# A two-layer hybrid decoder trunk on one core: the up product in its own buffer, and the probabilities' transposes and pooling products one step later

## The chip, the core and the metric

The kernel runs on one core of a Trainium2 chip. PE multiplies matrices, DVE and ACT work elementwise, GpSimd (POOL) does a few masks, and DMA queues move data, nearly all of them issued by SyncE (SP). Each engine takes its instructions in a fixed order and waits on semaphores for what other engines produce. The metric is the device time of one execution in microseconds (us); the time before is the median of three runs.

## The reference

Two layers run over 256 tokens of width 1024, all in float32. Cut to what matters here:

```python
def swiglu(x, w_gate, w_up, w_down):
    return (jax.nn.silu(x @ w_gate) * (x @ w_up)) @ w_down
...
for i in range(DEPTH):                                   # 2
    h = h + 0.5 * swiglu(rmsnorm(h, ffn1_norm[i]), ...)  # 1024 -> 2816 -> 1024
    u = rmsnorm(h, mix_norm[i])
    (q, c_kv, q_idx, w_idx, k_idx, x_pool, z, xbc, dt_raw, gate_raw) = jnp.split(u @ w_in[i], offs, axis=-1)
    y_attn = dsa_attention(...)   # indexer picks 64 of the causal keys; 8 heads: scores, softmax, values
    y_pool = pool_mixer(x_pool, pool_w[i], pool_scale[i])   # 4 groups: trailing mean minus x, times a 128x128 matrix
    y_ssd = ssd_mixer(...)        # convolution, chunked scan, gate
    merged = (g_attn * (y_attn @ w_br_attn[i]) + g_pool * (y_pool @ w_br_pool[i]) + g_ssd * (y_ssd @ w_br_ssd[i]))
    h = h + merged @ w_out[i]
    h = h + 0.5 * swiglu(rmsnorm(h, ffn2_norm[i]), ...)
    h = h + jax.nn.sigmoid(rmsnorm(h, ple_norm[i]) @ ple_w_gate[i]) * (p[i] @ ple_w_proj[i])
return rmsnorm(h, final_norm)
```

## The kernel before

Channels lie on partitions and tokens along the free dimension, so a product with 128 output channels is a matmul of a 128x128 weight tile against 128x256 activations. To keep float32 accuracy every operand is split into a high part and a low part of a shorter type (whi and wlo, uh and ul, gh and gl), and a product is the sum of three: high by high (L211), low of the activations by high of the weights (L212), high by low of the weights (L213).

Weights come in units of 128x1024. `load` (L141) issues the unit's transfer on SP into raw (L144), lets ACT cast the high part (L145) and DVE subtract it for the low part (L146). Raw has four buffers, whi and wlo five each. `unit` asks for a number of units ahead of the one in use (AHEAD, usually four). The low parts carry a mark ("turn"), and marked DVE instructions keep the order in which the program writes them. Everything else is put in order when the program is built, by a list scheduler that goes by its own estimates and by priorities; PE instructions issued through `self.mm` and `self.transpose` keep the program's order among themselves, other matmuls are placed freely. What results is one fixed order for each engine.

**FFN.** `ffn` goes over 22 pairs f of a gate and an up product, each of 24 matmuls, into the two halves of one PSUM bank (four banks called mm serve them in turn). For each pair DVE multiplies the gate product by the norm's factor (L494, out of PSUM), ACT takes a tanh (L498), DVE multiplies the same buffer by the up product (L500, out of PSUM, in place, after the tanh has read it), adds and multiplies (L501), and `split` makes gh and gl (L250, L251). A bank is free for a later pair when L500 has read it. In the very first FFN the norm's factor comes late (`todo`), so the first pairs wait together in a list. A small table there says how many units are asked for ahead of each unit.

**Mix.** Four generators are woven into one program: the state-space branch, the attention, the pooling branch and the gates' products. `weave` gives each a start, a number of steps and an end, and takes the next step from the one that is least far; a bare `yield` in a generator is an empty step that lets the others go on. In the attention `softmax` takes maxima (L896, DVE), exponentials (L898, ACT) and scalings of the probabilities (L902, ACT), lets 4 - h steps pass (h is the half of the queries), transposes them on PE (L114) and copies them out (L914). Where attention and state-space branch meet, `self.hold` is set to 4: that many of the next weight products (in groups of four tiles) are kept in program order behind what stands before them; others may be moved ahead by the scheduler. In the pooling branch each group's sum is split (L250, L251) and, two steps later, multiplied by its 128x128 matrix (po).

Of the kernel before, what the change touches and what calls it, by code (L numbers as in the profile page):

```python
# [13 lines left out]
OP = mybir.AluOpType  # L14
# [54 lines left out]
class Builder:  # L69
# [374 lines left out]
    def ffn(self, layer, u0, nxt, aside=None):  # L444
# [6 lines left out]
        for f in range(KF):  # L451
# [7 lines left out]
            elif f == 0:  # L459
                ps = [self.bank(t)[:, :S] for t in ("mm", "aux")]  # L460
                for c in range(KD):
                    for i, j in ((0, 0), (0, 1), (1, 0)):
                        for k, p in enumerate(ps):
                            nc.tensor.matmul(p, self.w01[i][:, c, k * P:(k + 1) * P], u[j][:, c],
                                             start=c + i + j == 0, stop=c == KD - 1 and i == 1)
                self.later()
                self.later()
            else:
                ps = self.bank()
                ps = [ps[:, :S], ps[:, S:]]  # L470
                for j in range(2):
                    n = 2 * f + j
                    ahead = self.AHEAD
                    if u0 == U_FFN1:
                        ahead = {2: 2, 3: 2, 4: 1}.get(n, ahead) if first else \
                            {2: 2, 3: 2}.get(n, ahead)
                    w = self.unit(layer, u0 + n, 1024, ahead=ahead)
                    keep = j == 0 and f == (2 if first else 1)
                    mid = u0 == U_FFN1 and n == (4 if first else 2)
                    if first and f < 4:  # L480
                        self.mmk_late(ps[j], w, u, keep, mid)
                    else:
                        self.mmk([(ps[j], w)], u, keep=keep, mid=mid)
# [5 lines left out]
            waiting.append((f, ps))  # L489
            if self.todo is None:  # L490
                for f1, p1 in waiting:
                    t = self.t([P, S], tag="t1")
                    with self.tc.high_priority(offset=160):
                        ins = nc.vector.tensor_tensor(t, p1[0], r, op=OP.mult)  # L494
                    if f1 == 0:
                        self.turn(ins)
                    th = self.t([P, S], tag="t1")
                    nc.scalar.activation(th, t, AF.Tanh, scale=0.5)  # L498
                    g = self.t([P, S], tag="t1")
                    nc.vector.tensor_tensor(t, t, p1[1], op=OP.mult)  # L500
                    nc.vector.scalar_tensor_tensor(g, th, 1.0, t, op0=OP.add, op1=OP.mult)  # L501
                    self.split(gh[:, f1], gl[:, f1], g)
                waiting = []
        self.new_u()
# [56 lines left out]
    def mix(self, layer, nxt):  # L561
# [180 lines left out]
                    yield from self.pool_group(layer, i + j, px[:, j], wpl, yp)  # L742

        with self.tc.issue_after(self.last.ins):
            self.weave((states(), 55, 1), (attend(), 36, 1), (pools(), 22, 0.88), (gate, 48, 1.1),
                       apart=(0, 1))
        ysh, ysl, rs = res["ssd"]

# [134 lines left out]
    def softmax(self, h, two, mb, out):  # L883
# [6 lines left out]
        for ps, _ in two:  # L890
# [11 lines left out]
                nc.scalar.mul(pr[:, j], pr[:, j], sums[:, j:j + 1])  # L902
            prs.append(pr)
            yield
        for _ in range(4 - h):
            yield
        pts = [self.bank("aux") for _ in prs]
        for pt, pr in zip(pts, prs):
            for j in range(4):
                self.transpose(pt[:, j * P:(j + 1) * P],  # L910
                               pr[:, j // nb, (j % nb) * P:(j % nb + 1) * P], self.ident)
        for (_, heads), pt in zip(two, pts):
            th = self.t([P, 4, P])
            nc.scalar.copy(th, pt.rearrange("p (a b) -> p a b", a=4))  # L914
            out.append((heads, th))
            yield
# [214 lines left out]
    def pool_group(self, layer, g, x, wpl, yp):  # L1131
# [16 lines left out]
        yh = self.t([P, S], FR, tag="t1")  # L1148
        yl = self.t([P, S], FR, tag="t1")
        self.split(yh, yl, y)  # L1150
        yield
        yield
        po = self.bank()
# [284 lines left out]
```

## Time and profile before

| | before |
|---|---|
| median of three runs | 1308.79 us (1307.43 to 1309.79) |
| the profiled execution | 1307.58 us, span 1305.7 us |
| granted TensorE clock | 0.999 |
| PE busy | 1295.8 us, 99% |
| DVE busy | 1048.6 us, 80% |
| ACT busy | 739.6 us, 57% |
| moved by DMA | 248.41 MB, mean 190 GB/s |

The page gives averages over the span. PE runs nearly without a gap, so the page alone tells little of a change of a few microseconds; the timelines of single stretches tell more. In them a row is: start in us, length in us, engine, line, operation, what is written from what, shape, how many in a row, and in brackets the idle time before it with what ended it.

### The profile page before, as it was taken

The page shows a single profiled execution, that of the slowest core. Times are in us where ns is not written, and L with a number is a line of the kernel's source. Part 1 is how long each engine was busy: PE and PEld are TensorE (multiplying, and loading weights), DVE is VectorE, ACT ScalarE, POOL GpSimd, SP SyncE. Part 2 cuts the span into 40 slices and gives each one's busy share as a digit, 9 for nine tenths or more (in the row PEclk, how much of TensorE's full clock was granted, in tenths as well). Part 3 has the DMA queues.
Part 4 walks back from the last instruction along what each step waited for, and adds up shares of the span by engine and source line. Part 5 has one row for each costly group of instructions (what it writes and reads, how often), then busy time and mean ns, then how long its engine had stood idle before and what let it go on. Part 6 is the DMA issues. An engine that isn't in the chain of part 4 may idle for free.

```text
span 1305.7 us, 28173 instructions
## 1 busy us (share of the span) xinstructions
PE 1295.8 (99%) x11468; PEld 1288.0 (99%) x11468; DVE 1048.6 (80%) x1919; ACT 739.6 (57%) x1203; POOL 7.0 (1%) x17
## 2 busy tenths in 40 slices
PE   9999999999999999999999999999999999999998
PEld 9999999999999999999999999999999999999997
DVE  7877669987999887766887776799789989777667
ACT  6555446656864555544655554566577646555455
POOL 0000000000000000000000000000000000000000
PEclk9999999999999999999999999999999999999999
DMA  7666656566546576666656666555555566666661
GB/s 267 212 194 194 195 166 207 181 189 206 171 159 217 166 225 195 194 194 194 194 178 207 192 196 192 162 195 187 189 199 167 176 203 212 195 194 195 194 192 66
DMA packets 72242, 248.41 MB, mean 190 GB/s; under 512 B 7920, under 2 KB 10416, under 8 KB 72112
## 3 DMA queue, kind: packets, MB, share of 16 engines
q1 hardware_dynamic: 71680, 245.82, 59.4%
q8 instruction: 90, 1.47, 0.5%
q10 hardware_dynamic: 432, 0.79, 0.2%
q14 instruction: 40, 0.33, 0.1%
HBM read 245.50 MB, written 1.08 MB: 189 GB/s over the span
## 4 chain that ended last, share of the span: by engine, by line
PE 97%; DVE 1%; DMA 1%; ACT 1%; issue 0%; SPq 0%; DVEq 0%; ACTq 0%
PE mm L212 30%; PE mm L213 30%; PE mm L211 30%; PE aux L111 3%; DMA raw<-in_w_dram 1%; PE aux L213 1%; PE aux L212 1%; PE aux L114 1%; PE aux L211 1%; DVE wlo L146 0%; PE mm L111 0%; PE mm L547 0%; ACT whi L145 0%; PE mm L247 0%; ACT t L343 0%
## 5 line engine op out<-in xcount | busy, mean ns | idle before, releaser
L145 ACT CAST whi<-raw 128x1024 fp32r<-128x1024 f32 (+1 forms) x456 | 475.0, 1045 | 472.2 <-issue 207.8
L146 DVE TENSOR_TENSOR wlo<-raw,whi 128x1024 fp32r<-128x1024 f32 (+1 forms) x456 | 551.5, 1214 | 179.9 <-ACT whi L145 178.7
L212 PE MATMUL mm<-ul,whi 128*128 128x256 f32 x2454 | 676.9, 277 | 0.0
L213 PE MATMUL mm<-uh,wlo 128*128 128x256 f32 x2454 | 676.6, 277 | 0.0
L211 PE MATMUL mm<-uh,whi 128*128 128x256 f32 x2419 | 667.2, 277 | 2.2 <-DVE t L500 2.2
L212 PEld LDWEIGHTS mm<-ul,whi 128*128 128x128 f32 x2454 | 460.6, 188 | 0.0
L213 PEld LDWEIGHTS mm<-uh,wlo 128*128 128x128 f32 x2454 | 459.8, 188 | 0.1
L211 PEld LDWEIGHTS mm<-uh,whi 128*128 128x128 f32 x2419 | 453.1, 188 | 2.9 <-DVE t L500 2.4
L213 PE MATMUL mm<-gh,wlo 128*128 128x256 f32 x704 | 194.4, 276 | 0.0
L212 PE MATMUL mm<-gl,whi 128*128 128x256 f32 x704 | 194.4, 276 | 0.0
L211 PE MATMUL mm<-gh,whi 128*128 128x256 f32 x704 | 193.9, 276 | 0.0
L213 PEld LDWEIGHTS mm<-gh,wlo 128*128 128x128 f32 x704 | 132.2, 188 | 0.0
L212 PEld LDWEIGHTS mm<-gl,whi 128*128 128x128 f32 x704 | 132.2, 188 | 0.0
L211 PEld LDWEIGHTS mm<-gh,whi 128*128 128x128 f32 x704 | 131.9, 188 | 0.0
L212 PE MATMUL mm<-a,whi 128*128 128x256 f32 x256 | 70.8, 276 | 0.0
L213 PE MATMUL mm<-a,wlo 128*128 128x256 f32 x256 | 70.8, 276 | 0.0
L211 PE MATMUL mm<-a,whi 128*128 128x256 f32 x256 | 70.7, 276 | 0.0
L211 PEld LDWEIGHTS mm<-a,whi 128*128 128x128 f32 x256 | 48.1, 188 | 0.0
L212 PEld LDWEIGHTS mm<-a,whi 128*128 128x128 f32 x256 | 48.1, 188 | 0.0
L213 PEld LDWEIGHTS mm<-a,wlo 128*128 128x128 f32 x256 | 48.1, 188 | 0.0
L494 DVE TENSOR_TENSOR t<-mm,rs_r 128x256 f32<-128x256 f32 x88 | 37.3, 423 | 9.8 <-PE mm L213 0.6
L501 DVE SCALAR_TENSOR_TENSOR t<-t,t 128x256 f32<-128x256 f32 x88 | 37.4, 425 | 2.9
(292 smaller groups left out, 1245.6 us busy)
## 6 DMA issues: line engine op xcount, KB each, us to landing
raw<-in_w_dram SPq DMA_DIRECT2D x446, 512.0 KB, 4.3
gh<-rates SPq DMA_DIRECT2D x16, 256.0 KB, 4.1
raw<-in_w_dram SPq DMA_DIRECT2D x8, 352.0 KB, 3.0
a<-in_x_dram SPq DMA_DIRECT2D x3, 512.0 KB, 5.7
gh<-rates SPq DMA_DIRECT2D x8, 128.0 KB, 4.6
out_dram<-uh SPq DMA_DIRECT2D x3, 256.0 KB, 2.0
a<-in_x_dram SPq DMA_DIRECT2D x1, 544.0 KB, 3.8
raw<-in_w_dram SPq DMA_DIRECT2D x2, 256.0 KB, 3.2
```

What stands on the lines that cost most here:

```text
L111: self.tc.keep_in_program_order(self.nc.tensor.matmul(*args, **kw))
L114: self.tc.keep_in_program_order(self.nc.tensor.transpose(*args))
L145: nc.scalar.copy(hi[:, :n], raw[:, :n])
L146: ins = nc.vector.tensor_tensor(lo[:, :n], raw[:, :n], hi[:, :n].bitcast(F), op=OP.subtract)
L211: (self.mm if keep else mm)(ps, a[0], b[0], start=start, stop=False)
L212: mm(ps, a[0], b[1], start=False, stop=False)
L213: mm(ps, a[1], b[0], start=False, stop=stop)
L494: ins = nc.vector.tensor_tensor(t, p1[0], r, op=OP.mult)
L501: nc.vector.scalar_tensor_tensor(g, th, 1.0, t, op0=OP.add, op1=OP.mult)
```

## The change

Three things change in the program:

- In the FFN, the up product gets a buffer of its own (g): it is issued right after the gate's product, with the same raised priority, and no longer waits for the tanh. For the first pair (in the first FFN, the first two) both products carry the "turn" mark. In the first FFN the table asks for two units ahead, not four, from unit 5 on (the second unit of pair 2), so that two low parts rather than four stand ahead of the first pairs' products on DVE.
- In the mix, one more empty step stands ahead of each block of probabilities' transposes (5 - h for 4 - h), and `hold` is raised to at least 1 behind them, so that the next weight product stays behind the transposes.
- One more empty step stands ahead of each pooling product, and the weights of `weave` follow: 39 steps for 36, and 26 steps up to 0.9 for 22 up to 0.88.

```diff
--- before.py
+++ after.py
@@ -472,7 +472,7 @@
                     n = 2 * f + j
                     ahead = self.AHEAD
                     if u0 == U_FFN1:
-                        ahead = {2: 2, 3: 2, 4: 1}.get(n, ahead) if first else \
+                        ahead = {2: 2, 3: 2, 4: 1, 5: 2}.get(n, ahead) if first else \
                             {2: 2, 3: 2}.get(n, ahead)
                     w = self.unit(layer, u0 + n, 1024, ahead=ahead)
                     keep = j == 0 and f == (2 if first else 1)
@@ -489,16 +489,14 @@
             waiting.append((f, ps))
             if self.todo is None:
                 for f1, p1 in waiting:
-                    t = self.t([P, S], tag="t1")
+                    t, th, g = (self.t([P, S], tag="t1") for _ in range(3))
                     with self.tc.high_priority(offset=160):
-                        ins = nc.vector.tensor_tensor(t, p1[0], r, op=OP.mult)
-                    if f1 == 0:
-                        self.turn(ins)
-                    th = self.t([P, S], tag="t1")
+                        ins = [nc.vector.tensor_tensor(t, p1[0], r, op=OP.mult),
+                               nc.vector.tensor_tensor(g, t, p1[1], op=OP.mult)]
+                    for x in ins if f1 < (2 if first else 1) else ():
+                        self.turn(x)
                     nc.scalar.activation(th, t, AF.Tanh, scale=0.5)
-                    g = self.t([P, S], tag="t1")
-                    nc.vector.tensor_tensor(t, t, p1[1], op=OP.mult)
-                    nc.vector.scalar_tensor_tensor(g, th, 1.0, t, op0=OP.add, op1=OP.mult)
+                    nc.vector.scalar_tensor_tensor(g, th, 1.0, g, op0=OP.add, op1=OP.mult)
                     self.split(gh[:, f1], gl[:, f1], g)
                 waiting = []
         self.new_u()
@@ -742,7 +740,7 @@
                     yield from self.pool_group(layer, i + j, px[:, j], wpl, yp)
 
         with self.tc.issue_after(self.last.ins):
-            self.weave((states(), 55, 1), (attend(), 36, 1), (pools(), 22, 0.88), (gate, 48, 1.1),
+            self.weave((states(), 55, 1), (attend(), 39, 1), (pools(), 26, 0.9), (gate, 48, 1.1),
                        apart=(0, 1))
         ysh, ysl, rs = res["ssd"]
 
@@ -902,13 +900,14 @@
                 nc.scalar.mul(pr[:, j], pr[:, j], sums[:, j:j + 1])
             prs.append(pr)
             yield
-        for _ in range(4 - h):
+        for _ in range(5 - h):
             yield
         pts = [self.bank("aux") for _ in prs]
         for pt, pr in zip(pts, prs):
             for j in range(4):
                 self.transpose(pt[:, j * P:(j + 1) * P],
                                pr[:, j // nb, (j % nb) * P:(j % nb + 1) * P], self.ident)
+        self.hold = max(self.hold, 1)
         for (_, heads), pt in zip(two, pts):
             th = self.t([P, 4, P])
             nc.scalar.copy(th, pt.rearrange("p (a b) -> p a b", a=4))
@@ -1150,6 +1149,7 @@
         self.split(yh, yl, y)
         yield
         yield
+        yield
         po = self.bank()
         s = slice(g * P, (g + 1) * P)
         self.mm3(po[:, :S], (wpl[0][:, s], wpl[1][:, s]), (yh, yl), True, True)
```

**DVE at the start of the first FFN.** The rows are from the first low part of pair 3 on; wlo is a low part of the weights, mm_16 and aux_17 the gate and up product of pair 0, mm_28 of pair 1, mm_35 of pair 2. Before:

```order
L146 TENSOR_TENSOR wlo_40_332<-raw_38_330,whi_39_331 128x1024
L146 TENSOR_TENSOR wlo_43_338<-raw_41_336,whi_42_337 128x1024
L146 TENSOR_TENSOR wlo_46_344<-raw_44_342,whi_45_343 128x1024
L146 TENSOR_TENSOR wlo_49_350<-raw_47_348,whi_48_349 128x1024
L494 TENSOR_TENSOR t1_50_380<-mm_16_155,rs_r_15_154 128x256
L146 TENSOR_TENSOR wlo_62_410<-raw_60_408,whi_61_409 128x1024
L500 TENSOR_TENSOR t1_50_380<-t1_50_380,aux_17_156 128x256
L146 TENSOR_TENSOR wlo_65_440<-raw_63_438,whi_64_439 128x1024
L501 SCALAR_TENSOR_TENSOR t1_52_384<-t1_51_382,t1_50_380 128x256
L494 TENSOR_TENSOR t1_53_389<-mm_28_232,rs_r_15_154 128x256
L146 TENSOR_TENSOR wlo_72_480<-raw_70_478,whi_71_479 128x1024
L251 TENSOR_TENSOR gl_6_98<-t1_52_384,gh_5_97 128x256
```

With the change:

```order
L146 TENSOR_TENSOR wlo_40_332<-raw_38_330,whi_39_331 128x1024
L146 TENSOR_TENSOR wlo_43_338<-raw_41_336,whi_42_337 128x1024
L494 TENSOR_TENSOR t1_44_368<-mm_16_155,rs_r_15_154 128x256
L495 TENSOR_TENSOR t1_46_370<-t1_44_368,aux_17_156 128x256
L494 TENSOR_TENSOR t1_47_377<-mm_28_232,rs_r_15_154 128x256
L499 SCALAR_TENSOR_TENSOR t1_46_370<-t1_45_369,t1_46_370 128x256
L495 TENSOR_TENSOR t1_49_379<-t1_47_377,mm_28_232 128x256
L494 TENSOR_TENSOR t1_50_386<-mm_35_293,rs_r_15_154 128x256
L146 TENSOR_TENSOR wlo_56_398<-raw_54_396,whi_55_397 128x1024
L146 TENSOR_TENSOR wlo_59_404<-raw_57_402,whi_58_403 128x1024
L499 SCALAR_TENSOR_TENSOR t1_49_379<-t1_48_378,t1_49_379 128x256
L495 TENSOR_TENSOR t1_52_388<-t1_50_386,mm_35_293 128x256
```

The two products of pairs 0 and 1 and the gate's of pair 2 now stand ahead of pair 4's low parts. The up product (L500, now L495) stands next to its gate product.

**PE at the same place.** mm_69 is pair 4 and mm_79 pair 5. With the change:

```order
L223 MATMUL mm_53_395<-uh_2_94,wlo_43_338 128x256 x8
L211 MATMUL mm_69_477<-uh_2_94,whi_55_397 128x256
L212 MATMUL mm_69_477<-ul_3_95,whi_55_397 128x256
L211 MATMUL mm_79_547<-uh_2_94,whi_61_409 128x256
L212 MATMUL mm_79_547<-ul_3_95,whi_61_409 128x256
L213 MATMUL mm_69_477<-uh_2_94,wlo_56_398 128x256
L211 MATMUL mm_69_477<-uh_2_94,whi_55_397 128x256
L212 MATMUL mm_69_477<-ul_3_95,whi_55_397 128x256
L213 MATMUL mm_69_477<-uh_2_94,wlo_56_398 128x256
```

Before, all 48 matmuls of pair 4 stood ahead of the first of pair 5; now two of pair 5 stand right behind the first two of pair 4.

**PE at the first probabilities' transposes (layer 0).** aux_630 and aux_631 take the transposes of t2_606 and t2_612 (t2_609 and t2_612 with the change); mm_616, mm_633, mm_634 and mm_639 are products of the next weights and mm_638 one of the pooling products. Before:

```order
L211 MATMUL mm_634_4451<-uh_388_2713,whi_618_4353 128x256
L212 MATMUL mm_634_4451<-ul_389_2714,whi_618_4353 128x256
L114 MATMUL aux_630_4436<-ident_75,t2_606_4292 128x128 x4
L213 MATMUL mm_634_4451<-uh_388_2713,wlo_619_4354 128x256
L211 MATMUL mm_634_4451<-uh_388_2713,whi_618_4353 128x256
L212 MATMUL mm_634_4451<-ul_389_2714,whi_618_4353 128x256
L213 MATMUL mm_634_4451<-uh_388_2713,wlo_619_4354 128x256
L211 MATMUL mm_634_4451<-uh_388_2713,whi_618_4353 128x256
L212 MATMUL mm_634_4451<-ul_389_2714,whi_618_4353 128x256
L211 MATMUL mm_638_4482<-t1_628_4420,whi_531_3768 128x256
L211 MATMUL mm_639_4488<-uh_388_2713,whi_602_4241 128x256
L212 MATMUL mm_639_4488<-ul_389_2714,whi_602_4241 128x256
```

and some rows on follow the other four, one at a time. With the change:

```order
L211 MATMUL mm_616_4351<-uh_388_2713,whi_592_4152 128x256
L212 MATMUL mm_616_4351<-ul_389_2714,whi_592_4152 128x256
L213 MATMUL mm_616_4351<-uh_388_2713,wlo_593_4153 128x256
L114 MATMUL aux_630_4437<-ident_75,t2_609_4299 128x128 x4
L114 MATMUL aux_631_4438<-ident_75,t2_612_4328 128x128 x4
L111 MATMUL mm_633_4449<-uh_388_2713,whi_598_4210 128x256
L212 MATMUL mm_633_4449<-ul_389_2714,whi_598_4210 128x256
L213 MATMUL mm_633_4449<-uh_388_2713,wlo_599_4211 128x256
L211 MATMUL mm_633_4449<-uh_388_2713,whi_598_4210 128x256
L212 MATMUL mm_633_4449<-ul_389_2714,whi_598_4210 128x256
```

Before, 25 matmuls of mm_634 stood between the last of mm_616 and the first transpose; now all eight transposes stand right behind mm_616. Layer 1 has the same order in both kernels.

**ACT at the same place.** L902 (now L900) scales the probabilities. Before:

```order
L898 ACTIVATE t2_612_4328,sum_614_4330<-t2_612_4328,mx_613_4329 128x128 x4
L254 ACTIVATE a8_540_3884<-mm_620_4372,cc0_90 128x256
L145 CAST whi_618_4353<-raw_617_4352 128x1024
L902 ACTIVATE t2_606_4292<-t2_606_4292,sum_608_4294 128x128 x4
L250 CAST t1_628_4420<-t1_627_4418 128x256
L902 ACTIVATE t2_612_4328<-t2_612_4328,sum_614_4330 128x128 x4
L145 CAST whi_624_4399<-raw_623_4398 128x1024
L683 ACTIVATE gh_345_2476<-mm_616_4351 128x512
L145 CAST whi_636_4453<-raw_635_4452 128x1024
```

With the change:

```order
L896 ACTIVATE t2_609_4299,sum_611_4301<-t2_609_4299,mx_610_4300 128x128 x4
L896 ACTIVATE t2_612_4328,sum_614_4330<-t2_612_4328,mx_613_4329 128x128 x4
L254 ACTIVATE a8_540_3884<-mm_620_4372,cc0_90 128x256
L145 CAST whi_618_4353<-raw_617_4352 128x1024
L900 ACTIVATE t2_609_4299<-t2_609_4299,sum_611_4301 128x128 x4
L900 ACTIVATE t2_612_4328<-t2_612_4328,sum_614_4330 128x128 x4
L250 CAST t1_628_4420<-t1_627_4418 128x256
L145 CAST whi_624_4399<-raw_623_4398 128x1024
L681 ACTIVATE gh_345_2476<-mm_616_4351 128x512
```

The cast L250 has moved from between the scalings to behind them; the cast of weights (L145) stays ahead of them.

**ACT at the third block of probabilities (second half of the queries).** With the change:

```order
L896 ACTIVATE t2_697_4879,sum_699_4881<-t2_697_4879,mx_698_4880 128x256 x2
L896 ACTIVATE t2_709_4928,sum_711_4930<-t2_709_4928,mx_710_4929 128x256 x2
L254 ACTIVATE a8_540_3884<-mm_704_4908,cc0_90 128x256
L145 CAST whi_702_4891<-raw_701_4890 128x1024
L900 ACTIVATE t2_697_4879<-t2_697_4879,sum_699_4881 128x256 x2
L900 ACTIVATE t2_709_4928<-t2_709_4928,sum_711_4930 128x256 x2
L145 CAST whi_716_4961<-raw_715_4960 128x1024
```

Before, whi_702 stood behind the four scalings; now it stands ahead of them. On PE the transposes of this block stood as four, two and two with matmuls between, and now stand as eight in a row.

## The prediction

> **What bounds the kernel now.** I read the page first.
>
> ```profile
> span 1305.7 us, 28173 instructions
> ...
> PE 1295.8 (99%) x11468; PEld 1288.0 (99%) x11468; DVE 1048.6 (80%) x1919; ACT 739.6 (57%) x1203; POOL 7.0 (1%) x17
> ...
> PE 97%; DVE 1%; DMA 1%; ACT 1%; issue 0%; SPq 0%; DVEq 0%; ACTq 0%
> ```
>
> PE is busy in 99% of the span and holds 97% of the chain that ended last. PE takes its instructions in the written order, so the change matters only where PE comes to wait, or waits less. The view of waits on PE names three:
>
> ```profile
> PE mm L211 <- DVE t L500: 2.2, 1, 2.2
> PE aux L114 <- ACT uh L1300: 1.9, 1, 1.9
> PE aux L169 <- DVE onesr L411: 1.3, 1, 1.3
> ```
>
> Only the first lies where the change works. Short waits show as gaps between the starts of neighbouring matmuls in the timeline; a 128x256 matmul starts every 0.113 us when nothing is late (349.08 to 349.19 below).
>
> **First FFN: a wait that mostly goes.** The timelines of PE, DVE and ACT there:
>
> ```profile
> 34.15 0.28 PE L213 MATMUL mm<-uh,wlo 128*128 128x256 f32 x1
> 36.67 0.39 PE L211 MATMUL mm<-uh,whi 128*128 128x256 f32 x1 [2.24 <-DVE t L500]
> 36.89 0.28 PE L212 MATMUL mm<-ul,whi 128*128 128x256 f32 x1
> ...
> 23.63 4.62 DVE L146 TENSOR_TENSOR wlo<-raw,whi 128x1024 fp32r<-128x1024 f32 x4
> 28.17 0.42 DVE L494 TENSOR_TENSOR t<-mm,rs_r 128x256 f32<-128x256 f32 x1
> 36.20 0.42 DVE L500 TENSOR_TENSOR t<-t,mm 128x256 f32<-128x256 f32 x1
> ...
> 28.54 1.05 ACT L145 CAST whi<-raw 128x1024 fp32r<-128x1024 f32 x1 [2.21 <-DMA raw<-in_w_dram]
> ```
>
> PE should go on at 34.15 + 0.11 = 34.26, starts at 36.67 and needs 0.22 instead of 0.11 for the next step: 2.41 + 0.11 = 2.5 us are lost. It waits for the bank that the up product of pair 1 (L500, 36.20) still reads; DVE came to it late, behind four low parts in a row and behind a tanh. In the change two low parts stand ahead (half of 4.62: until about 25.95), then five short products and sums of 0.42 at most: the up product of pair 1 ends by about 28.0. PE now has pair 5's first two matmuls right behind pair 4's first two, at 28.78 + 2 x 0.11 = 29.0 by the old times. The bank is free then, but the high part for them is the cast of 28.54, which ends at 29.59 and began when its transfer landed. So a shorter wait takes its place: 29.6 + 0.05 - 29.0 = 0.65, with the restart 0.76. Gain 2.51 - 0.76 = **1.75 us**. Bounds: 2.5 if the transfer lands sooner, 1.0 if pair 4's first low part comes 0.75 after PE asks for it.
>
> What else moves there: SP issues the two 0.11 MB constant loads ahead of pair 4's transfers instead of behind; at the 275 GB/s moved in this stretch that is 0.8 us on pair 4's weights, whose second half PE needs only at about 32.4. Pair 4's first low part, behind the short products, is ready at about 29.3, and PE asks for it at 29.87: 0.5 us of cover; without it the price is what it is late. In the other FFNs DVE does the same two products of 0.42 per pair in another order; PE stays covered by weights that are split over a microsecond ahead: nothing.
>
> **The first probabilities: a new wait.** The timelines of PE and ACT at the transposes of the first half of the queries:
>
> ```profile
> 327.69 0.28 PE L213 MATMUL mm<-uh,wlo 128*128 128x256 f32 x1
> ...
> 330.64 0.60 PE L114 MATMUL aux<-ident,t 128*128 128x128 f32 x4
> ...
> 333.06 0.27 PE L114 MATMUL aux<-ident,t 128*128 128x128 f32 x1
> ...
> 328.01 1.05 ACT L145 CAST whi<-raw 128x1024 fp32r<-128x1024 f32 x1
> 328.95 1.28 ACT L902 ACTIVATE t<-t,sum 128x128 f32<-128x128 f32 x4
> 330.13 0.40 ACT L250 CAST t<-t 128x256 fp32r<-128x256 f32 x1
> 330.42 1.29 ACT L902 ACTIVATE t<-t,sum 128x128 f32<-128x128 f32 x4
> ```
>
> Each transpose needs one of the eight scalings (L902). Before, PE runs 25 matmuls of the next weights from 327.81 on, then the four transposes at 330.64, after the fourth scaling ended (328.95 + 1.28 = 330.23), and the last four one by one until 333.06, each behind its scaling. In the change these 25 matmuls stand behind all eight transposes (held), so PE reaches the first transpose at about 327.7. A step later in the generator's own order is therefore earlier on PE, because the next matmuls no longer fill the time. ACT's order hardly changes: exponentials, L254, the same cast, then eight scalings in a row, 0.29 apart (1.28 less the last one's 0.41, over three). They begin at 328.95 at best; the product that feeds the chain of scans and maxima ahead of the exponentials stands four matmuls (0.45 us) later on PE, of which I count 0.2, as the casts behind it close up. Last scaling: 328.95 + 0.2 + 7 x 0.29 + 0.41 = 331.6. The eighth transpose starts at 331.7, the next weights at 331.8. Unhindered they would start at 327.7 + 8 x 0.11 = 328.6. **Loss 3.2 us.** Bounds: 2.1, if the 1.05 cast does not stand ahead of the scalings; 3.6, if the whole 0.45 and another short ACT instruction of 0.2 come on top. A gain is excluded as long as the transposes stand in front of the 25 matmuls, for nothing on PE is left to run before them.
>
> Layer 1 has the same order and the same times from start to start:
>
> ```profile
> 972.77 1.28 ACT L902 ACTIVATE t<-t,sum 128x128 f32<-128x128 f32 x4
> ...
> 974.50 0.60 PE L114 MATMUL aux<-ident,t 128*128 128x128 f32 x4
> ```
>
> 1.73 us from scaling to transposes against 1.69 in layer 0, so twice 3.2 = **+6.4**.
>
> For the second block the transposes already stand together:
>
> ```profile
> 349.08 0.28 PE L212 MATMUL mm<-ul,whi 128*128 128x256 f32 x1
> 349.19 0.28 PE L213 MATMUL mm<-uh,wlo 128*128 128x256 f32 x1
> 349.31 1.04 PE L114 MATMUL aux<-ident,t 128*128 128x128 f32 x8
> 350.11 0.36 PE L211 MATMUL mm<-uh,whi 128*128 128x256 f32 x1
> ```
>
> Eight in a row cost 0.11 each; a change between the two types costs no more than some 0.05 (0.20 from 350.11 to the next start). Joining the split blocks saves 0.06 us per layer. The scalings of this block stay over 2 us ahead: nothing.
>
> **Pooling product and third block.** PE, DVE and ACT:
>
> ```profile
> 360.07 0.28 PE L211 MATMUL mm<-t,whi 128*128 128x256 f32 x1
> ...
> 362.01 0.28 PE L212 MATMUL mm<-ul,whi 128*128 128x256 f32 x1
> 362.31 0.39 PE L212 MATMUL mm<-t,whi 128*128 128x256 f32 x1
> ...
> 366.77 0.60 PE L114 MATMUL aux<-ident,t 128*128 128x128 f32 x4
> ...
> 367.45 0.38 PE L114 MATMUL aux<-ident,t 128*128 128x128 f32 x2
> ...
> 361.85 0.40 DVE L251 TENSOR_TENSOR t<-t,t 128x256 fp32r<-128x256 f32 x1
> ...
> 365.77 1.71 ACT L902 ACTIVATE t<-t,sum 128x256 f32<-128x256 f32 x4 [0.29 <-DVE sum L900]
> 367.39 1.03 ACT L145 CAST whi<-raw 128x1024 fp32r<-128x1024 f32 x1
> ```
>
> The product of the pooled low part starts 0.30 instead of 0.11 behind its neighbour: it waits 0.2 for L251. Now 12 instead of 17 matmuls stand between the first part of that product (360.07) and this one, so PE comes 5 x 0.113 = 0.57 earlier to a DVE chain of the same length: **+0.55 per layer**; bounds -0.3 (the old wait goes, where DVE catches up during the stall above) and +1.0. In the third block all eight transposes stand in one piece, and the cast of 1.03 has moved ahead of the four scalings (in pairs of transposes, 0.41 apart). The scalings then start at about 366.35 instead of 365.77 and end at 368.06 instead of 367.48 (old times), while PE asks for the last pair at about 367.35 instead of 367.90: the last two transposes wait 0.75, that is **+0.75 per layer**; bounds 0, where the cast runs in a gap, and 1.2, where another 0.4 of ACT comes between.
>
> **Sum.** -1.75 + 2 x (3.2 + 0.55 + 0.75 - 0.06) = -1.75 + 8.9 = +7.1 us. The profiled execution took 1307.58 (span 1305.7 plus 1.9 around it), 1.2 under the median of the runs, so 1314.7 beside it and **1315.9** beside 1308.79: 0.54% slower. With all bounds on one side the sum is -2.5 + 2 x (2.1 - 0.3 + 0 - 0.06) = +1.0, and -1.0 + 2 x (3.6 + 1.0 + 1.2) = +10.6.
>
> **Rivals.**
> 1. *Only the first block stalls.* DVE and ACT use the 3.2 us to get ahead, so that the pooling product and the third block find their inputs ready: -1.75 + 6.4 - 0.1 = +4.5, 1313.3. For it: ACT is busy 57%. Against: between the two blocks ACT and DVE hang on PE's scores.
> 2. *The first FFN gains nothing*, because pair 5 meets its low part or pair 4's instead: +8.9, 1317.7. For it: DVE is full from 23.6 to 37 and four low parts follow. Against: they have to be there only from 29.9 on.
> 3. *The clock drops in the new wait.* In 327.7 to 331.8 PE would run only transposes, 0.3 apart. Rows for and against:
>
> ```profile
> 1.32 4.47 PE L169 MATMUL aux<-onesr 128*128 128x512 f32 x10 [1.32 <-DVE onesr L411]
> 5.73 0.38 PE L464 MATMUL mm<-uh,gh 128*128 128x256 f32 x1
> 34.00:37.00 3.00, 0.76 (x6) 0.56 (x6) 2.97 (x6) 2.10 (x3) 0.00 (x0) 1.00 0.86 285
> ```
>
> The first ten matmuls take 4.41 us from 1.32 to 5.73, where 20 widths of 256 at 0.113 would take 2.3: PE is slow after standing still, by 2.1 us. After the wait of 2.2 in 34 to 37 the granted clock is 1.00 and the pace full. If the new wait brings the slow pace back once per layer, 7.1 + 2 x 2.1 = +11.3, 1320.1. The Trainium skill, "TensorE: Matmul & The Clock Gate", Part 1, puts the return to half rate at about 3.4 us without work, and its Part 4 says that transposes don't count as busy; by that rule this stall, of 4.1 us from matmul to matmul, would be long enough, and the trace, which has none so long, can't tell.
> 4. *Faster: the scalings are done in time.* The point that decides is whether the eighth scaling ends before PE wants the eighth transpose, at 328.5 by the old times. It would have to come 3.1 us earlier, with the exponentials at 321 instead of 324: only if DVE's maxima ran ahead of the scans there. Then the old short waits go as well: -1.75 - 2 x 0.3 - 0.1 = -2.45, 1306.3, with the full FFN gain 1305.6. Against, from the busy times by stretch:
>
> ```profile
> 318.00:331.00 13.00, 13.00 (x133) 12.76 (x134) 12.44 (x40) 9.57 (x31) 0.00 (x0) 1.00 0.62 212
> ```
>
> DVE is busy 12.44 of 13 us there, so it has nothing to bring forward.
>
> **How the numbers follow.** Chances: forecast 0.50, rival 1 0.20, rival 2 0.12, rival 3 0.08, rival 4 0.10. A measurement of this kernel tells about 0.2% (2.6 us) from no change. The first four cases are slower by more than that, but smaller stalls than I bound them could leave 0.03 of them within it; rival 4 lies at the edge and is shared, 0.06 faster and 0.04 same. So slower 0.87, same 0.07, faster 0.06. The range leaves out rival 4 and half of rival 3: 1310.5 to 1320, where the low end is the sum of small first stalls (2.1) and no later ones, and the runs' own spread of some 1.2.
>
> **What would show it.** Right: the wait of PE on L500 is gone and a wait of some 0.65 on a cast (L145) stands near 29; the transposes of the first block wait for the scalings (now L900) in both layers, some 3 us in all from the first to the last, and the next weights start right behind; gaps of 0.7 to 0.9 at the pooling product and the third block. Wrong: transposes of the first block at the pace of 0.11, or no loss between 320 and 345 against the old timeline; a granted clock under 1.00 there would be rival 3; a wait over 2 us near 29 to 36 would be rival 2.

## The result, and the profile after

The change makes the kernel slower: 1317.12 us median of six executions (1314.54 to 1317.73) beside 1309.36 for the kernel before, a ratio of 1.0059 with a 95% interval of 1.0048 to 1.0070. The profiled execution took 1314.54, 6.96 more than the profiled one before; the forecast was 7.1 more. Four executions further below took 1438 to 4782 us (three of the run with the table's entry alone, one of the kernel before beside the first four runs) and are left out of all ratios. The page and the view of waits on PE of the changed kernel:

```profile
PE 1301.0 (99%) x11468; PEld 1288.8 (98%) x11468; DVE 1047.2 (80%) x1919; ACT 739.8 (56%) x1203; POOL 7.0 (1%) x17
...
PE aux L114 <- ACT t L900: 3.7, 2, 1.9
PE mm L211 <- ACT whi L145: 0.3, 1, 0.3
```

The wait on L500 is gone from the list. In its place stands a short one on a cast (L145), and a new one of 3.7 us in two pieces: the transposes (L114) wait for the scalings of the probabilities (now L900), once in each layer. PE's busy share still reads 99%, as before.

To see where the time goes, the same PE instruction is found in both timelines: a transpose at the start of each layer's mix, the eight transposes of the second block, and a product with a column of ones at the mix's end. Before (the second block of layer 0 starts at 349.31):

```profile
295.13 0.27 PE L114 MATMUL aux<-ident,t 128*128 128x128 f32 x1
385.51 0.39 PE L111 MATMUL aux<-t,onesr 128*128 128x256 f32 x2
938.93 0.27 PE L114 MATMUL aux<-ident,t 128*128 128x128 f32 x1
993.20 1.04 PE L114 MATMUL aux<-ident,t 128*128 128x128 f32 x8
1029.32 0.39 PE L111 MATMUL aux<-t,onesr 128*128 128x256 f32 x2
```

With the change:

```profile
292.95 0.27 PE L114 MATMUL aux<-ident,t 128*128 128x128 f32 x1
350.52 1.04 PE L114 MATMUL aux<-ident,t 128*128 128x128 f32 x8
387.90 0.39 PE L111 MATMUL aux<-t,onesr 128*128 128x256 f32 x2
941.29 0.27 PE L114 MATMUL aux<-ident,t 128*128 128x128 f32 x1
998.85 1.04 PE L114 MATMUL aux<-ident,t 128*128 128x128 f32 x8
1036.24 0.40 PE L111 MATMUL aux<-t,onesr 128*128 128x256 f32 x2
```

The differences of these starts, taken from one mark to the next:

| stretch | forecast | measured |
|---|---|---|
| up to the mix of layer 0 | -1.75 | -2.18 |
| layer 0, to the second block's transposes | +3.1 to +3.2 | +3.39 |
| layer 0, rest of the mix | +1.2 to +1.3 | +1.18 |
| between the mixes | 0 | -0.03 |
| layer 1, to the second block's transposes | +3.1 to +3.2 | +3.29 |
| layer 1, rest of the mix | +1.2 to +1.3 | +1.27 |
| sum | +7.1 | +6.9 |

**First FFN.** PE, DVE and ACT with the change:

```profile
28.64 0.28 PE L212 MATMUL mm<-ul,whi 128*128 128x256 f32 x1
29.20 0.39 PE L211 MATMUL mm<-uh,whi 128*128 128x256 f32 x1 [0.28 <-ACT whi L145]
29.43 0.28 PE L212 MATMUL mm<-ul,whi 128*128 128x256 f32 x1
...
27.05 0.41 DVE L495 TENSOR_TENSOR t<-t,mm 128x256 f32<-128x256 f32 x1
...
28.10 1.05 ACT L145 CAST whi<-raw 128x1024 fp32r<-128x1024 f32 x1 [0.85 <-DMA raw<-in_w_dram]
```

Pair 5's first matmul starts 0.45 late (29.20 less 28.64 and a step of 0.11) and the next step takes 0.12 more: 0.56 lost where 2.51 were. The up product of pair 1 (L495) ends at 27.46, long before; the cast ends at 29.15, and its transfer set its start.

**First probabilities.** PE and ACT with the change, and PE in layer 1:

```profile
325.49 0.28 PE L213 MATMUL mm<-uh,wlo 128*128 128x256 f32 x1
327.63 2.37 PE L114 MATMUL aux<-ident,t 128*128 128x128 f32 x8 [1.86 <-ACT t L900]
329.76 0.36 PE L111 MATMUL mm<-uh,whi 128*128 128x256 f32 x1
...
327.17 2.45 ACT L900 ACTIVATE t<-t,sum 128x128 f32<-128x128 f32 x8
...
975.95 2.37 PE L114 MATMUL aux<-ident,t 128*128 128x128 f32 x8 [1.87 <-ACT t L900]
```

The last matmul ahead starts at 325.49 and the next weights at 329.76, 4.27 later; one step and eight transposes at full pace take 1.0, so 3.3 us are lost: 2.0 until the first scaling is done, and 1.3 because each transpose then comes 0.29 behind the last, at the pace of the scalings.

**Rest of the mix.** PE, DVE and ACT around the third pooling product, the third block, and the fourth pooling product; last, PE before, at the block of values that the fourth product now stands in:

```profile
362.64 0.28 PE L213 MATMUL mm<-uh,wlo 128*128 128x256 f32 x1
362.95 0.38 PE L212 MATMUL mm<-t,whi 128*128 128x256 f32 x1
...
367.53 1.64 PE L114 MATMUL aux<-ident,t 128*128 128x128 f32 x8
...
373.12 0.28 PE L213 MATMUL mm<-uh,wlo 128*128 128x256 f32 x1
...
374.34 0.39 PE L212 MATMUL mm<-t,whi 128*128 128x256 f32 x1
...
376.92 0.36 PE L111 MATMUL mm<-uh,whi 128*128 128x256 f32 x1
...
362.49 0.40 DVE L251 TENSOR_TENSOR t<-t,t 128x256 fp32r<-128x256 f32 x1
...
366.96 1.71 ACT L900 ACTIVATE t<-t,sum 128x256 f32<-128x256 f32 x4
...
371.46 0.28 PE L213 MATMUL mm<-uh,wlo 128*128 128x256 f32 x1
374.53 0.36 PE L111 MATMUL mm<-uh,whi 128*128 128x256 f32 x1
```

The third pooling product still starts 0.31 behind its neighbour, as before, and not later. The third block's eight transposes wait 0.2 for the first scaling and then take until 368.92, 0.5 longer than at full pace. And the fourth pooling product's low parts now stand in the middle of the block of values (374.34). From the last weights ahead of that block to the first behind it take 3.80 us (373.12 to 376.92), where they took 3.07 before (371.46 to 374.53); the two matmuls more are worth 0.23 of this, so 0.5 is lost.

### The profile page after: what moved, and what is told of

Read it like the earlier page. It is cut to its first block, busy times and chain, and to the rows that moved or that the text cites. A ratio compares the mean times of both kernels' runs of the same rounds, so it can differ in the third digit from the quotient of the medians.

```text
span 1312.6 us, 28337 instructions
## 1 busy us (share of the span) xinstructions
PE 1301.0 (99%) x11468; PEld 1288.8 (98%) x11468; DVE 1047.2 (80%) x1919; ACT 739.8 (56%) x1203; POOL 7.0 (1%) x17
## 4 chain that ended last, share of the span: by engine, by line
PE 95%; ACT 2%; DVE 2%; DMA 1%; issue 0%; SPq 0%; DVEq 0%; ACTq 0%
PE mm L212 29%; PE mm L213 29%; PE mm L211 29%; PE aux L111 2%; PE aux L114 1%; PE aux L213 1%; PE aux L212 1%; DMA raw<-in_w_dram 1%; PE aux L211 1%; DVE wlo L146 1%; ACT whi L145 1%; ACT t L896 0%; PE mm L545 0%; PE mm L111 0%; DVE ct L1071 0%
## 5 line engine op out<-in xcount | busy, mean ns | idle before, releaser
L145 ACT CAST whi<-raw 128x1024 fp32r<-128x1024 f32 (+1 forms) x456 | 475.3, 1044 | 486.6 <-PE mm L212 369.7
L495 DVE TENSOR_TENSOR t<-t,mm 128x256 f32<-128x256 f32 x87 | 36.5, 419 | 2.7
```

Source lines behind the costliest of these rows:

```text
L145: nc.scalar.copy(hi[:, :n], raw[:, :n])
L495: nc.vector.tensor_tensor(g, t, p1[1], op=OP.mult)]
```

## The experiments

**One part at a time.** Four kernels: only the FFN part; the whole change without the line that raises hold; the FFN part and that line alone, without the empty steps; only the mix part.

```diff
 e1: kernel before, with the first two hunks of the change alone
 e2: the change, without
-        self.hold = max(self.hold, 1)
 e3: e1, with
+        self.hold = max(self.hold, 1)
 e4: the change, without its first two hunks
```

Expected of the FFN part alone: 

> Only the FFN part of the change: the up product in its own buffer and two low parts ahead in the first FFN; the mix is as before. My account: the wait on L500 (2.4 us and a restart of 0.1) is replaced by a wait of 0.45 and 0.1 on a cast, as in the profile of the whole change, so about 1.9 us less than before: 1307.5 beside 1309.4, and no other wait. Rival: the two parts of the change hang together, the FFN part also shifts weights' casts in the mix, and part of the loss shows here: 1310 or more.

Measured: 1305.89 us median (1305.41 to 1307.53) beside 1309.27 before, ratio 0.9978 (0.9969 to 0.9987). The profiled execution took 1305.52, 2.06 less than the profiled one before, as foretold; and the mix keeps its old times (54.30 and 36.14 us for the first table's two stretches of layer 0, 54.18 and 36.20 before). But the medians lie 3.4 apart, 1.5 more than the wait was worth. This stayed open until the clock was looked at, below.

Expected without hold: 

> The whole change without the line that raises hold behind the transposes; the empty steps and the weights of the weave stay. My account: the written order puts the first transposes behind 25 matmuls of the next weights again (the same place as before), so the two stalls of 2.0 us and the slow pace of the transposes behind them (1.3 us) are gone: between 1.0 and 2.3 us less than before, 1307 to 1308.4. Rival: the empty steps and the new order on ACT and DVE make the loss, and it stays: 4 to 8 us more than before.

Measured: 1306.78 (1306.44 to 1307.20), ratio 0.9984 (0.9975 to 0.9993), 2.5 us less than before, just beyond what I expected. So hold is what makes the change slow: one line less is worth 10 us of the median, and the empty steps alone cost 0.9 beside the FFN part.

Expected of hold without the empty steps: 

> The FFN part and the line that raises hold, without the empty steps and with the old weights of the weave. My account: this line alone puts all eight transposes ahead of the 25 matmuls, so each layer loses 2.9 to 3.3 us at the first block and 0.3 to 0.4 at the third; with the FFN's gain 4.5 to 5.5 us more than before: 1314 to 1315. It does not split the block of values with a pooling product, so it stays under the whole change by up to 0.9. Rival (the empty steps make the loss): 1.9 us less than before.

Measured: 1328.65 (1327.77 to 1329.64), 19.4 more than before, ratio 1.0151 (1.0136 to 1.0165). My account was right that the line alone makes the stall, and far off in the size. The views of waits and the timeline of PE at the third block:

```profile
PE aux L114 <- ACT t L900: 3.7, 4, 1.6
PE mm L212 <- DVE t L251: 3.6, 4, 1.5
PE mm L211 <- ACT t L250: 3.5, 2, 1.8
...
372.14 0.38 PE L211 MATMUL mm<-t,whi 128*128 128x256 f32 x1 [1.76 <-ACT t L250]
374.07 0.58 PE L212 MATMUL mm<-t,whi 128*128 128x256 f32 x1 [1.54 <-DVE t L251]
```

Without the empty steps the fourth pooling product stands right behind the third block's transposes, and hold keeps the next weights behind both. PE finds nothing else to do and waits for the product's high and low part, 1.8 and 1.5 us, in both layers. So the steps are not idle: beside hold they keep this second stall away. The clock adds to it: the granted clock is 0.50 from 373 to 379.7, and all four executions have a mean of 0.992 or 0.993. The next run shows what that is.

Expected of the mix part alone: 

> Only the mix part of the change, the FFN as before. My account: the sum is additive, so 1.9 us more than the whole change: 9 to 9.7 us more than before, 1318.5 to 1319. Rival (the parts hang together): the same as the whole change within 1 us.

Measured: 1322.18 (1320.80 to 1323.46), 12.9 more than before, ratio 1.0101 (1.0085 to 1.0116); 3 more than additive parts would give. Its profile shows why. PE, and the busy times by stretch (the third figure from the end is the granted clock):

```profile
34.05 0.28 PE L213 MATMUL mm<-uh,wlo 128*128 128x256 f32 x1
36.74 0.58 PE L211 MATMUL mm<-uh,whi 128*128 128x256 f32 x1 [2.42 <-DVE t L500]
...
37.00:40.00 3.00, 3.00 (x15) 3.00 (x16) 2.96 (x7) 0.75 (x2) 0.00 (x0) 0.50 0.76 274
...
333.93 0.42 PE L212 MATMUL mm<-ul,whi 128*128 128x256 f32 x1
334.14 0.41 PE L213 MATMUL mm<-uh,wlo 128*128 128x256 f32 x1
...
333.50:337.00 3.50, 3.50 (x18) 3.50 (x18) 3.24 (x7) 3.23 (x6) 0.00 (x0) 0.51 0.39 142
```

Behind the wait on L500 and behind the transposes the granted clock is 0.50 and 0.51 for some 3 us, and matmuls start every 0.213 us instead of 0.113: 13 or 14 of them, which with the slower first step loses some 1.5 us each time. This is the third rival of the prediction, the clock that drops behind a new wait. In this execution it came behind three waits (layer 1 the third); in the profiled executions of the kernel before and of the change it came behind none of them.

**Is it the clock, and is it PE's standing still?** Four kernels: the change again; the change with hold for the second half alone; a longer and a shorter stall with PE's order unaltered.

```diff
 e6
-        self.hold = max(self.hold, 1)
+        self.hold = max(self.hold, h)
 e7, behind the scalings
+            for j in range(per if h == 0 and prs else 0):
+                nc.scalar.mul(pr[:, j], pr[:, j], 1.0)
 e8
-                nc.scalar.mul(pr[:, j], pr[:, j], sums[:, j:j + 1])
+                if h == 0 and prs:
+                    nc.vector.tensor_scalar(pr[:, j], pr[:, j], sums[:, j:j + 1], None, op0=OP.mult)
+                else:
+                    nc.scalar.mul(pr[:, j], pr[:, j], sums[:, j:j + 1])
```

Expected of the change again: 

> The whole change once more, unaltered. In its six timed executions the mean granted clock was 0.999 once (1314.54, the profiled one) and 0.996 to 0.998 otherwise (1315.8 to 1317.7). My account: in those the clock falls after the first probabilities' transposes, as in the profile of the mix part alone, where 15 matmuls behind the stall start every 0.213 us instead of 0.113, which costs 1.6 us in a layer. So the times gather near 1314.5, 1316.1 and 1317.7 for no, one and two falls, and a profile with a mean clock under 0.999 shows a stretch of some 3.4 us at about half the clock right behind the transposes near 330 or 978. Rival: the spread has another cause (transfers, say) and such a profile shows full pace there.

Measured: 1315.62 (1314.86 to 1317.42), ratio 1.0052 (1.0039 to 1.0065). With the first six there are now eleven executions, and they gather nearly as foretold, the lower the mean granted clock the longer: two at 1314.5 and 1314.9 with 0.999, four from 1315.5 to 1315.9 with 0.998, five from 1317.1 to 1317.7 with 0.996 or 0.997. The profiled one (1315.86, 0.998) shows a short fall behind the transposes of layer 0, five matmuls of 0.213, and none in layer 1. (Every profiled execution, of whatever kernel, ends with 1.6 to 4.5 us at half clock, when PE has little or nothing left to do. This alone takes the mean to 0.999 or 0.998, so 0.998 may or may not hold a fall.)

Expected of hold for the second half alone: 

> The whole change, but hold is raised only for the second half of the queries (h = 1); in the first half the 25 matmuls stand ahead of the transposes again. My account: both stalls at the first block and all falls of the clock go; the third block keeps its eight transposes in a row, with a wait of 0.4 or less: 1306.5 to 1308, times close together. Rival: holding is dear wherever it is done, and the third block or the pooling product ahead of it then waits 1 us or more per layer: 1309 or more.

Measured: 1309.69 (1309.61 to 1311.90), ratio 1.0008 (0.9999 to 1.0017). The first block's stalls are gone, and nine of eleven executions lie within 0.3 us with a clock of 0.999. But the rival holds as well; PE at the third pooling product of layer 0:

```profile
359.68 0.28 PE L213 MATMUL mm<-uh,wlo 128*128 128x256 f32 x1
360.63 0.39 PE L212 MATMUL mm<-t,whi 128*128 128x256 f32 x1 [0.68 <-DVE t L251]
```

It now starts 0.95 behind its neighbour instead of 0.31, and layer 1 has the same wait. That is the +0.55 that the prediction had put there (0.64 here), and that the whole change did not show: there PE comes later, after its stall, and DVE has caught up. Holding the second half alone costs 2.9 beside no hold at all; my account of 1306.5 to 1308 was too low.

Expected of the longer stall: 

> The whole change with four needless scalings by one behind the last four scalings of the first half, which gives the same result. On ACT they come behind a cast, an activation and a copy, so the eighth transpose starts some 3.3 us later in each layer; PE's order is unaltered. My account: 6.6 us more for the two longer stalls, and the clock falls in both layers in every execution, another 3.2 over the execution without falls: 1323 to 1326, mean clock 0.996 or lower throughout. Rival (the clock has no part): 1314.5 + 6.6 = 1321 with a clock of 0.999 in some executions.

Measured: 1324.46 (1323.85 to 1324.87), ratio 1.0117 (1.0103 to 1.0131), mean clock 0.993 or 0.994 in all executions. The next weights start 3.1 us later behind the stall in each layer, and the clock falls in both: 21 and 13 matmuls at 0.213, 3.4 us in all. As expected by the account with the clock; more than 3 us over the one without.

Expected of the shorter stall: 

> The whole change with the last four of the eight scalings of the first half done by DVE, which has them ready before ACT's first four end. PE's order is unaltered. My account: the first four transposes still come every 0.29 us, the last four every 0.11, so the stall is 0.7 us shorter per layer: 1.4 us under the whole change where the clock stays (1313.1), and the clock falls less often, so the median is 2 to 4 us under that of the whole change. Rival (the wait is not for the scalings): within 0.5 us of the whole change.

Measured: 1316.31 (1314.68 to 1316.85), ratio 1.0051 (1.0039 to 1.0064): no better than the change, and half of my expectation fails. PE at the first block of layer 0 and the stretch behind:

```profile
327.79 1.65 PE L114 MATMUL aux<-ident,t 128*128 128x128 f32 x8 [1.86 <-ACT t L903]
329.19 0.37 PE L111 MATMUL mm<-uh,whi 128*128 128x256 f32 x1
...
329.30:333.00 3.70, 3.70 (x21) 3.70 (x20) 3.09 (x7) 2.63 (x5) 0.00 (x0) 0.54 0.55 176
```

The stall is 0.73 shorter, as foretold (1.40 from the first transpose to the next weights instead of 2.13). But the clock falls at least as often: 0.54 here, and once more in layer 1; none of the five executions has a mean of 0.999. 3.5 us without a matmul of weights is as bad as 4.3 here. The times fit 1313.1 with one fall (1314.7) and with two (1316.3).

**The stall filled.** The decisive test leaves the stall where it is and gives PE needless work in it.

```diff
         pts = [self.bank("aux") for _ in prs]
+        for _ in range(8 if h == 0 else 0):
+            self.mm(pts[0], self.onesr, self.onesr[:, None, :].to_broadcast([P, 4, P]),
+                    start=True, stop=True)
```

Expected: 

> The whole change with eight needless matmuls (128x512, ones, into the bank that the transposes then overwrite) right ahead of the first transposes of the first half, in both layers. At 0.23 us each they take 1.8 of the 2.0 us in which PE waits there for the first scaling, so the transposes and all behind them start when they did. My account (the clock falls because PE does nearly nothing for some 4 us): no falls there any more, the matmuls behind the transposes start every 0.113 us, and the times gather at 1314.5 to 1315 with a clock of 0.999. Rival (the falls have nothing to do with PE's idle time): 1314.5 to 1317.7 as without them, with clocks of 0.996 to 0.998.

Measured: 1314.86 (1314.59 to 1315.01), ratio 1.0044 (1.0030 to 1.0058). PE, and the stretch behind:

```profile
325.96 1.99 PE L111 MATMUL aux<-onesr 128*128 128x512 f32 x8
328.00 2.37 PE L114 MATMUL aux<-ident,t 128*128 128x128 f32 x8
330.12 0.36 PE L111 MATMUL mm<-uh,whi 128*128 128x256 f32 x1
...
330.00:334.00 4.00, 4.00 (x36) 3.96 (x36) 3.43 (x7) 4.00 (x7) 0.00 (x0) 1.00 0.43 144
```

The transposes start when they did, the clock stays at 1.00 behind them, and all five executions lie within 0.42 us at the change's fastest. So the falls come from PE's standing still ahead of the transposes. (The one profile would not show it, for the change's first profile has no fall either; the five times together do.) Without them the mix part costs 9.0 us over the FFN part (1314.86 less 1305.89), and 9.1 by the marks of the first table (3.39 + 1.18 + 3.29 + 1.27).

**When it falls.** In the five profiled executions with falls in mid-span, every fall lasts 3.41 us or twice that, and the distances between their edges are whole multiples of 3.413 us (with hold alone, 12 of them from 331.96, where one fall ends, to 372.92, where the next begins). So in these traces the granted clock is set on a beat of 3.413 us, which lies differently to the program in each execution. The busy times by beat, two beats each of the change again, where the clock falls, and of the change's first profile, where it stays:

```profile
324.54:327.95 3.41, 1.57 (x13) 1.29 (x12) 3.09 (x10) 3.41 (x13) 0.00 (x0) 1.00 0.22 65
327.95:331.36 3.41, 3.41 (x15) 2.67 (x15) 1.99 (x5) 3.41 (x11) 0.00 (x0) 0.50 0.70 237
...
327.10:330.51 3.41, 2.88 (x14) 1.81 (x15) 1.79 (x3) 3.41 (x11) 0.00 (x0) 1.00 0.69 205
330.51:333.92 3.41, 3.41 (x32) 3.41 (x31) 2.89 (x7) 3.41 (x7) 0.00 (x0) 1.00 0.33 127
```

The first count is PE's instructions in the beat, 32 when it works on weights throughout. In all thirteen profiles a beat with at most 13 of them is followed by one at half clock, and a beat with 14 or more by one at full clock. The wait on L500 shows what the beat's position does: in the profile before, its emptiest beat (32.76 to 36.18) has 15 and the clock stays; in that of the mix part alone, with a wait 0.2 longer, the beat from 33.20 to 36.62 has 10 and the clock falls. Transposes count here: eight of the 14 in the change's beat are transposes, and one of the 13 in the beat before the fall.

**The FFN's two edits apart.**

```diff
 e10, kernel before with
-                        ahead = {2: 2, 3: 2, 4: 1}.get(n, ahead) if first else \
+                        ahead = {2: 2, 3: 2, 4: 1, 5: 2}.get(n, ahead) if first else \
 e11: kernel before, with the second hunk of the change alone
```

Expected of the table alone: 

> The kernel before with the table's entry alone: two low parts instead of four stand ahead of the first pairs' products in the first FFN; the up product stays in place behind the tanh. In the written order the up product of pair 1 still stands behind three more low parts and one of gl, about 1.3 us earlier than before. My account: the wait of pair 5 on L500 shrinks from 2.4 to about 1.1: 1.3 us less than before where the clock stays. Rival (the own buffer does nothing, the low parts are all): the whole 1.9 us.

Measured: 1306.02 us, median of its other seven executions (1305.88 to 1306.51), ratio 0.9980 (0.9970 to 0.9990). The wait is the foretold one:

```profile
PE mm L211 <- DVE t L500: 1.3, 1, 1.3
```

Expected of the own buffer alone: 

> The kernel before with the up product in its own buffer alone, and the marks; four low parts stay ahead of the first pairs' products. In the written order the up product of pair 1 ends near 30.3 and pair 5 starts only behind all of pair 4, at 34.2, so neither the bank nor the cast of pair 5's weights (29.6) is late. My account: no wait is left there, 2.5 us less than before, 0.5 less than the FFN part with the table: 1305.0 where the clock stays. Rival (without the table the four low parts keep the bank late): 0.5 us or more over the FFN part as a whole.

Measured: 1305.11 (1304.74 to 1306.71), ratio 0.9973 (0.9963 to 0.9982). No wait of PE is left there: the up product of pair 1 ends at 30.7, and PE asks for its bank only near 34. This is the fastest of all the kernels, 12 us under the change and 3.9 under the kernel before. Beside executions of the kernel before whose clock stays (1307.3 to 1308.1) it is some 2.5, as foretold.

## Why the prediction was right

**The first probabilities** carried the sum and came out right: 3.3 us lost in the stall for 3.2, and 3.39 and 3.29 in the two stretches. The order shows hold putting the transposes ahead of 25 matmuls, the trace before shows when the scalings end; the scalings of the change start at 327.17 and PE reaches the transposes at 325.60, 1.57 ahead, where the prediction had 329.15 less 327.7, 1.45. One word of the account goes too far. The prediction says that a step later in the generator's order is therefore earlier on PE; but it is hold alone that does this. With the empty steps and without hold (e2) the first four transposes stand together again and the others come one at a time (328.67 to 330.88); with hold and without the steps (e3) all eight stand behind the stall (327.20 to 329.56).

**The first FFN** was forecast at 1.75 and gave 1.95 in the wait and 2.18 up to the mix; the other 0.23 was gained ahead of it, where pair 4's first matmul starts at 28.52 instead of 28.78. The step that was mis-sized is the cast that takes the place of L500: its transfer landed 0.4 earlier than taken (28.10 for 28.54); why was not tried. The cast was put at fault rightly, and e11 shows that without the table's entry there is no such wait at all.

**Rest of the mix** was right in its sum (1.2 per layer), and that in part by luck, for one term too many made up for one too few. The pooling product's +0.55 did not come, because DVE uses the stall to catch up: the low part's L251 starts 1.21 us behind the product's first matmul (361.28 to 362.49), where it started 1.78 behind it before (360.07 to 361.85). This is the first rival's argument, true of this place alone, and the wait does come where the stall is absent (e6). The third block's +0.75 came out: the ten steps from 367.25 to 369.12 take 1.87 us, 0.74 more than at 0.113 each, while the block in pieces had lost next to nothing (fifteen steps from 366.65 to 368.36 in 1.71). And the fourth pooling product in the block of values, for which the prediction has no term, costs 0.5. Why it costs that much was not tried. The three together also give what e6 shows, where nothing is caught up: 0.64 + 0.74 + 0.5 = 1.88, and its rest of the mix in layer 0 is 1.84 longer than before.

**The rivals.** The clock (rival 3) was given 0.08 and 2.1 us per layer. It happens in most executions of the change, not behind each stall, at 0.5 to 1.6 us each. It did not move the forecast out of its range, because the kernel before pays it too: of its 20 executions that e1 was compared with, those with a mean clock of 0.998 or more lie from 1307.3 to 1308.1, and those with 0.997 or less from 1309.1 to 1311.7. (The 35 beside the later runs leave a gap too, from 1308.4 to 1308.7, but five of the slower ones read 0.998.) I take these as falls behind the wait on L500, which e4's profile shows and the kernel before's one profile does not; that explains most of the 1.5 us by which the FFN part gained more in the median than its wait was worth. Two things speak for it. Laid over the trace before in every position, the beat has at most 13 instructions around this wait in some 55% of the positions (an estimate from that one trace), and 33 of the 55 executions took 1308.7 or more; and with the wait of 1.3 (e10), where no position has so few, seven executions lie within 0.7 us. Still it is argued, not shown: no execution of the kernel before with a low clock was profiled. And that its one profile shows full pace behind this wait, which the prediction held against the rival, was the luck of the beat. Against the account stands that the FFN part, without that wait, has three executions near 1307.4, two of them with a clock under 0.999; their cause is open.

The Trainium skill, "TensorE: Matmul & The Clock Gate", Part 1, has the clock return to half rate after an idle window of about 3.4 us, and to full rate after a busy one of about the same length. The half rate agrees (0.50 granted, 0.213 for 0.113), and so does the length (3.41 us). That the window has to be idle does not: e4 falls behind 2.7 us without a matmul (34.05 to 36.74), after a beat in which PE had 10 instructions, and the change again after one of 13. Its Part 4 says that transposes don't count as busy in the same way; the runs don't bear this out, for without its eight transposes the change's beat from 327.10 to 330.51 would have six instructions, and the clock stays.

## What to carry to other kernels

On an in-order engine that bounds the time, holding other work behind an instruction puts that instruction earlier on the engine and takes away the cover of its wait: count the instructions that stood ahead of it in the written order, and compare with the time at which its operands are ready. A stall of PE that leaves a beat of 3.41 us with 13 or fewer of 32 instructions, which takes some 2 us or more (19 of the 32 are 2.0 us, an estimate from these counts), can cost 0.5 to 2.1 us more through the clock (e5, e7), in some executions and not in others; so a short wait is worth more than its length. A mean granted clock of 0.997 or less over an execution as long as these tells that this has happened.

## What was not expected of the hardware

- The granted clock is set on a beat of 3.413 us: it was 0.50 behind every beat with at most 13 PE instructions and 1.00 behind every one with 14 or more, in thirteen profiles. So the same wait makes it fall in one execution (2.4 us in e4) and not in another (2.2 us before). With 7.3 us between matmuls of weights (e7) it fell in both layers.
- Eight needless matmuls in the stall kept the clock at 1.00 and narrowed the spread of the executions from 3.2 us to 0.4.
- Changing between float32 and the shorter type costs next to nothing where transposes stand among matmuls: before, eleven steps from 332.01 to 333.29 with four single transposes in them take 1.28 us, where 0.113 each would give 1.24. The step behind a transpose is long (0.20), but the step to it is short (0.03).
